# Row sums of relu(x): own semaphores, multi-row instructions and another split of memory in a kernel that streams 64 MB

## The chip, the cores and the metric

The kernel runs on one core of one Trainium2 chip. The metric is the device time of one execution in microseconds (us). A core has several engines with instruction queues of their own: ScalarE (ACT), VectorE (DVE), GpSimd (POOL), TensorE (PE, without work here) and SyncE (SP), which mostly issues DMAs. The transfers themselves are done by 16 DMA engines.

## The reference

```
x: float32 [32, 512, 1024]
relu_x = maximum(x, 0)
out    = sum(relu_x, axis=-1)      # float32 [32, 512]
```

There are 32 x 512 = 16384 rows of 1024 numbers, 4 KB each, 67.1 MB in all. Each row becomes one number: the sum of its positive parts.

## The kernel before

`trace_relu_sum` lays the rows over the 128 partitions so that partition p owns 128 rows that follow each other in memory (`xv`, `"(p m) d -> p (m d)"`). From one partition's data to the next one's it is 128 rows x 4 KB = 512 KB: the pitch. The rows of a partition are numbered m = 0 to 127.

They are loaded in pieces (`chunks`): seven blocks of 16 rows a partition (8.39 MB each), then a tail of 8, 4, 2 and 1 rows, and the last row (m = 127) in four column pieces of 244, 252, 260 and 268 numbers. All loads are issued by SP (line 95 for blocks and tail, line 121 for the pieces). The 16-row blocks and the 8-row tail share a pool of two buffers (tag `io`), so that a load waits until the block two before it has been worked off; the smaller ones have buffers of their own.

Each row is one instruction. Even rows go to ACT (`act_op`, line 71: Relu with an accumulated output), odd ones to DVE (`dve_op`, line 79: max with 0, then add, with an accumulated output). Both write one column of `res` (128 x 128). Each is followed by a short instruction that reads the accumulator. The four pieces of the last row are reduced by DVE; the first three sums are put behind the fourth piece's data, so that the fourth reduction gives the whole row.

The results leave in two stores: columns 0 to 125 from ACT's queue (line 103), and the last two columns from SP (line 128), at the end.

The tile framework places all semaphores and the closing: at the end (its instructions carry line 16) SP waits for the outstanding DMAs, and then all engines pass a barrier, GpSimd clears the semaphores, and all engines pass a second barrier. `issue_ahead_of_the_barrier` moves the first load on SP (`EARLY = 1`) in front of the barrier with which the program opens.

Of the kernel before, what the change touches and what calls it, by code (L numbers as in the profile page):

```python
# [1 line left out]

# [4 lines left out]

EARLY = 1  # L10


def kernel(tc: tile.TileContext, x: bass.AP, out: bass.AP):
    trace_relu_sum(tc, x, out)
    tc.close()
    tc.compile()  # L16
    issue_ahead_of_the_barrier(tc, EARLY)


def issue_ahead_of_the_barrier(tc: tile.TileContext, n_loads: int):  # L20


    SP = mybir.EngineType.SP
    blocks = tc.nc.main_func.blocks
    opening = blocks[0].instructions
    body = next(b for b in blocks if b.name == tc.start_bb_name).instructions
    loads = [i for i in body if i.engine == SP][:n_loads]
    for i in loads:
        assert isinstance(i, mybir.InstDMACopy)
        body.remove(i)  # L30
    at = next(
        n
        for n, i in enumerate(opening)
        if i.engine == SP and isinstance(i, mybir.InstDrain)
    )
    opening[at:at] = loads


@with_exitstack
def trace_relu_sum(  # L40
    ctx: ExitStack,
    tc: tile.TileContext,
    x: bass.AP,
    out: bass.AP,
):
    nc = tc.nc
    fp32 = mybir.dt.float32

    P = nc.NUM_PARTITIONS
    x_flat = x.flatten_outer_dims()  # L50
    N, D = x_flat.shape
    assert N % P == 0
    NT = N // P

    xv = x_flat.rearrange("(p m) d -> p (m d)", p=P)
    out2d = out.rearrange("b s -> (b s)").rearrange("(p m) -> p m", p=P)

    big = 16
    tail = [8, 4, 2, 1]
    pieces = [244, 252, 260, 268]  # L60
    assert sum(pieces) == D
    nbig, rem = divmod(NT - sum(tail) - 1, big)
    assert rem == 0
    chunks = [big] * nbig + tail

    io_pool = ctx.enter_context(tc.tile_pool(name="io", bufs=2))
    res_pool = ctx.enter_context(tc.tile_pool(name="res", bufs=1))
    res = res_pool.tile([P, NT], fp32)

    def act_op(in_ap, out_ap, m):  # L70
        nc.scalar.activation(  # L71
            out=out_ap,
            in_=in_ap,
            func=mybir.ActivationFunctionType.Relu,
            accum_out=res[:, m : m + 1],
        )

    def dve_op(in_ap, out_ap, accum_out):
        nc.vector.tensor_scalar(  # L79
            out=out_ap,  # L80
            in0=in_ap,
            scalar1=0.0,
            scalar2=None,
            op0=mybir.AluOpType.max,
            op1=mybir.AluOpType.add,
            accum_out=accum_out,
        )

    m0 = 0
    for j, cpd in enumerate(chunks):  # L90
        if cpd >= 8:
            xt = io_pool.tile([P, cpd, D], fp32, tag="io", name=f"xt{j}")
        else:
            xt = io_pool.tile([P, cpd, D], fp32, tag=f"t{cpd}", bufs=1, name=f"xt{j}")
        nc.sync.dma_start(  # L95
            out=xt,
            in_=xv[:, m0 * D : (m0 + cpd) * D].rearrange("p (c d) -> p c d", c=cpd),
        )
        for c in range(cpd):
            m = m0 + c  # L100
            if m == NT - 2:
                act_op(xt[:, c, :], xt[:, c, :], m)
                nc.scalar.dma_start(out=out2d[:, 0 : NT - 2], in_=res[:, 0 : NT - 2])
            elif (c % 2) == 0:
                act_op(xt[:, c, :], xt[:, c, :], m)
            else:
                dve_op(xt[:, c, :], xt[:, c, :], res[:, m : m + 1])
        m0 += cpd

    m_last = m0  # L110
    assert m_last == NT - 1
    base = m_last * D
    np_ = len(pieces)
    wlast = pieces[-1] + (np_ - 1)
    ptiles = []
    col = 0
    for i, w in enumerate(pieces):
        shape_w = w if i < np_ - 1 else wlast
        pt = io_pool.tile([P, shape_w], fp32, tag=f"p{i}", bufs=1, name=f"p{i}")
        ptiles.append(pt)  # L120
        nc.sync.dma_start(out=pt[:, 0:w], in_=xv[:, base + col : base + col + w])
        col += w
    last = ptiles[-1]
    for i in range(np_ - 1):
        dve_op(ptiles[i], ptiles[i], last[:, pieces[-1] + i : pieces[-1] + i + 1])
    dve_op(last, last, res[:, m_last : m_last + 1])

    nc.sync.dma_start(out=out2d[:, NT - 2 : NT], in_=res[:, NT - 2 : NT])


# [1 line left out]
_INS = ['x']  # L132
_OUTS = [((32, 512), 'float32')]


# [23 lines left out]
```

## Time and profile before

| | us |
|---|---|
| median of 8 runs | 163.48 (163.25 to 163.70) |
| the profiled execution's own time | 163.87 |
| its span, from the first to the last instruction | 162.1 |
| DVE busy | 74.2 |
| ACT busy | 69.0 |
| POOL busy | 0.2 |
| a row on DVE (128x1024) | 1.215 each |
| a row on ACT (128x1024) | 1.043 each |

The span is shorter than the time of the execution it comes from, since something lies around the first and last instruction (here 1.77 us). Shares on the page are of the span. "q1" is the DMA queue that SP issues to, "q10" that of ACT, and "q14" brings instructions. The profiled execution is one execution; the median is that of unprofiled ones.

When the blocks have arrived can be read from the starts of the first ACT instruction of each, which waits for the transfer. These are lines of the trace's timeline, ACT alone (start, length, instruction, and in brackets how long the engine had been idle and what ended it):

```
22.36 1.06 ACT L71 ACTIVATE xt<-xt 128x1024 f32<-128x1024 f32 x1 [20.29 <-DMA xt<-in_x_dram]
41.69 1.06 ACT L71 ACTIVATE xt<-xt 128x1024 f32<-128x1024 f32 x1 [10.91 <-DMA xt<-in_x_dram]
61.59 1.06 ACT L71 ACTIVATE xt<-xt 128x1024 f32<-128x1024 f32 x1 [11.48 <-DMA xt<-in_x_dram]
80.97 1.06 ACT L71 ACTIVATE xt<-xt 128x1024 f32<-128x1024 f32 x1 [10.95 <-DMA xt<-in_x_dram]
100.82 1.06 ACT L71 ACTIVATE xt<-xt 128x1024 f32<-128x1024 f32 x1 [11.43 <-DMA xt<-in_x_dram]
120.17 1.06 ACT L71 ACTIVATE xt<-xt 128x1024 f32<-128x1024 f32 x1 [10.93 <-DMA xt<-in_x_dram]
139.53 1.06 ACT L71 ACTIVATE xt<-xt 128x1024 f32<-128x1024 f32 x1 [10.93 <-DMA xt<-in_x_dram]
149.24 1.06 ACT L71 ACTIVATE xt<-xt 128x1024 f32<-128x1024 f32 x1 [1.29 <-DMA xt<-in_x_dram]
```

### The profile page before, as it was taken

Reading aid. Unit: us, or ns where it says so; the run is one execution under the profiler, and the core shown is the slowest. Engines: PE = TensorE matmul, PEld = TensorE weight load, DVE = VectorE, ACT = ScalarE, POOL = GpSimd, SP = SyncE. Lnnn points to the kernel's source line nnn. Section 1 sums busy time; section 2 is a strip of 40 time slices with the busy share of each in tenths; the row PEclk is TensorE's granted clock in tenths of the full one; section 3 lists DMA queues with packets and bytes.
Section 4 is the critical chain, followed back from the end, with each engine's and each line's share of the span. In section 5 each row is a group of like instructions: output and inputs, shape, how many; then the busy total and the mean of one; then the engine's idle time right before and its main releaser. Section 6 shows DMA issues by size and latency. Waiting matters only on the chain.

```text
span 162.1 us, 347 instructions
## 1 busy us (share of the span) xinstructions
DVE 74.2 (46%) x134; ACT 69.0 (43%) x129; POOL 0.2 (0%) x4
## 2 busy tenths in 40 slices
DVE  0000049700795007940099201991039900598983
ACT  3000049500793007920099001990039700596882
POOL 0000000000000000000000000000000000000000
DMA  7996997997997998998998999999999997998980
GB/s 259 518 485 291 518 501 307 485 501 307 485 518 291 485 469 372 453 469 372 453 487 374 437 469 404 421 469 421 404 485 404 404 501 332 421 453 384 416 334 22
DMA packets 2450, 67.19 MB, mean 415 GB/s; under 512 B 528, under 2 KB 1040, under 8 KB 1168
## 3 DMA queue, kind: packets, MB, share of 16 engines
q1 hardware_dynamic: 2304, 67.11, 96.7%
q10 hardware_dynamic: 144, 0.06, 0.1%
q14 instruction: 2, 0.02, 0.0%
HBM read 67.11 MB, written 0.07 MB: 414 GB/s over the span
## 4 chain that ended last, share of the span: by engine, by line
DMA 79%; DVE 18%; SPq 1%; issue 0%; DVEq 0%
DMA xt<-in_x_dram 62%; DVE xt L79 17%; DMA p<-in_x_dram 17%; SPq L95 1%; DVE p L79 1%; DVEq L79 0%; DVEq L16 0%
## 5 line engine op out<-in xcount | busy, mean ns | idle before, releaser
L79 DVE TENSOR_SCALAR_CACHE_REDUCE xt<-xt 128x1024 f32<-128x1024 f32 x63 | 72.6, 1215 | 85.1 <-DMA xt<-in_x_dram 84.8
L71 ACT ACTIVATE xt<-xt 128x1024 f32<-128x1024 f32 x64 | 66.7, 1043 | 89.6 <-DMA xt<-in_x_dram 89.6
L71 ACT ACTIVATION_READ_ACCUMULATOR xt<-xt 128x1 f32 x64 | 12.0, 187 | 0.0
L79 DVE DVE_READ_ACCUMULATOR xt<-xt 128x1 f32 x63 | 5.2, 83 | 0.0
L79 DVE TENSOR_SCALAR_CACHE_REDUCE p<-p 128x244 f32<-128x244 f32 (+3 forms) x4 | 1.6, 420 | 0.4 <-DMA p<-in_x_dram 0.4
L71 ACT ACT_TABLE_LOAD x1 | 1.3, 1283 | 0.8 <-PEq L143 0.8
L79 DVE DVE_READ_ACCUMULATOR p<-p 128x1 f32 x4 | 0.3, 82 | 0.0
L143 POOL MEMSET const-bfloat16-1.0<- 128x1 bf16 x1 | 0.1, 101 | 0.0
L143 POOL MEMSET const-uint8-127<- 128x1 uint8 x1 | 0.1, 101 | 0.0
L143 POOL MEMSET const-float32-0.0<- 128x1 f32 x1 | 0.1, 98 | 0.2 <-issue 0.2
L143 POOL MEMSET const-float32-1.0<- 128x1 f32 x1 | 0.1, 98 | 0.0
## 6 DMA issues: line engine op xcount, KB each, us to landing
xt<-in_x_dram SPq DMA_DIRECT2D x1, 4096.0 KB, 19.7
xt<-in_x_dram SPq DMA_DIRECT2D x1, 2048.0 KB, 24.2
xt<-in_x_dram SPq DMA_DIRECT2D x1, 1024.0 KB, 26.2
xt<-in_x_dram SPq DMA_DIRECT2D x1, 512.0 KB, 27.0
p<-in_x_dram SPq DMA_DIRECT2D x1, 134.0 KB, 10.0
p<-in_x_dram SPq DMA_DIRECT2D x1, 130.0 KB, 26.5
p<-in_x_dram SPq DMA_DIRECT2D x1, 126.0 KB, 26.7
p<-in_x_dram SPq DMA_DIRECT2D x1, 122.0 KB, 26.8
```

What stands on the lines that cost most here:

```text
L71: nc.scalar.activation(out=out_ap, in_=in_ap, func=mybir.ActivationFunctionType.Relu, accum_out=res[:, m : m + 1],)
L79: nc.vector.tensor_scalar(out=out_ap, in0=in_ap, scalar1=0.0, scalar2=None, op0=mybir.AluOpType.max, op1=mybir.AluOpType.add, accum_out=ac ...
L95: nc.sync.dma_start(out=xt, in_=xv[:, m0 * D : (m0 + cpd) * D].rearrange("p (c d) -> p c d", c=cpd),)
L143: nc = _bacc.Bacc("TRN2", target_bir_lowering=False, num_devices=1)
```

## The change

The computation stays the same; nearly the whole kernel is written anew.

- The framework's context is closed at once, and its body is filled with instructions that carry semaphores of the kernel's own: one for each of the 15 loads, one that ACT counts up, one that DVE counts up, and one for the stores.
- Memory is split in two. The first 2048 rows (8 MB) are the first block, in which a partition owns 16 rows (pitch 16 x 4 KB = 64 KB). The remaining 14336 rows are laid out with 112 rows a partition (pitch 448 KB). The loads keep their sizes: seven blocks of 16 rows, a tail of 8, 4, 2, 1, and four pieces.
- There are three buffers of 16 rows instead of two. The load of block j waits for DVE's count after block j-3; the tail's four loads share one buffer and only the first of them waits.
- Blocks 0 to 5 are worked off in multi-row instructions: ACT writes relu over n rows in place (`clamp`), then DVE sums these n rows with one `tensor_reduce` (`total`), which waits for ACT. The groups are 16, 16, 16, 8+8, 8+8, 6+5 rows. The other 5 rows of block 5 are single rows on ACT; block 6 is 8 single rows on ACT and 8 on DVE; the tail alternates as before.
- There are three stores, all on SP: the first block's 16 columns, then 110 columns, then the last two. The first two are issued after all loads in SP's program.
- At the end only GpSimd waits for the stores (semaphore at 48) and runs two of its closing instructions, among them the clear; the other closing instructions are dropped.

```diff
 def tile_relu_sum_kernel(tc: tile.TileContext, x: bass.AP, out: bass.AP):
-    trace_relu_sum(tc, x, out)
+    nc = tc.nc
+    sems = Semaphores(tc)
+
     tc.close()
     tc.compile()
+    nc.cur_bb = nc.bb_map[tc.start_bb_name]
+    body = nc.cur_bb.bb.instructions
+    ends = list(body)
+    body.clear()
+    n_stores = relu_sum(nc, sems, x, out)
+    body.extend(ends)
+
+    nc.cur_bb = nc.bb_map[tc.start_bb_name + "_end"]
+    body = nc.cur_bb.bb.instructions
+    clear = semaphore_clear(body)
+    body.clear()
+    nc.gpsimd.wait_ge(sems.stored, 16 * n_stores)
+    body.extend(clear)
     issue_ahead_of_the_barrier(tc, EARLY)
...
+TWO = [[16], [16], [16], [8, 8], [8, 8], [6, 5], []]
+ACT = [0, 0, 0, 0, 0, 5, 8]
+DVE = [0, 0, 0, 0, 0, 0, 8]
...
+    xf = x_flat[:N1].rearrange("(p m) d -> p m d", p=P)
+    xv = x_flat[N1:].rearrange("(p m) d -> p m d", p=P)
...
+    def store(m, n, act, dve):
+        nonlocal n_store
+        dst, src = sums(m, n)
+        nc.sync.wait_ge(sems.act, act)
+        nc.sync.dma_start(out=dst, in_=src).wait_op(sems.dve, dve, "sem-ge").then_inc(
+            sems.stored, 16
+        )
+        n_store += 1
+
+    def clamp(ap, loaded):
+        nonlocal n_act
+        i = nc.scalar.activation(out=ap, in_=ap, func=RELU)
+        if loaded is not None:
+            i.wait_op(loaded, 16, "sem-ge")
+        i.then_inc(sems.act, 1)
+        n_act += 1
+
+    def total(ap, m, n):
+        nonlocal n_dve
+        nc.vector.tensor_reduce(
+            out=res[:, m : m + n], in_=ap, axis=mybir.AxisListType.X, op=ADD
+        ).wait_op(sems.act, n_act, "sem-ge").then_inc(sems.dve, 1)
+        n_dve += 1
...
+    for j in range(NB):
+        buf = bufs[j % NBUF]
+        loaded = load(buf[:, :, :], rows(m, ROWS), j >= NBUF and freed[j - NBUF])
+        c = 0
+        act_waits = dve_waits = loaded
+        for n in TWO[j]:
+            clamp(buf[:, c : c + n, :], act_waits)
+            total(buf[:, c : c + n, :], m + c, n)
+            act_waits = None
+            c += n
+        for _ in range(ACT[j]):
+            act_row(buf[:, c, :], m + c, act_waits)
...
+        for _ in range(DVE[j]):
+            dve_row(buf[:, c, :], res[:, m + c : m + c + 1], dve_waits)
...
+        freed.append((n_act, n_dve))
...
+    store(0, ROWS, *freed[0])
+    store(ROWS, NT - ROWS - 2, n_act - 1, n_dve)
...
+    store(NT - 2, 2, n_act, n_dve)
+    return n_store
+
+
+def semaphore_clear(instructions):
+
+    pool = [i for i in instructions if i.engine == mybir.EngineType.Pool]
+    at = next(
+        n for n, i in enumerate(pool) if getattr(i, "is_reset_sema", False)
+    )
+    return pool[at : at + 2]
```

`act_row` and `dve_row` are the single-row instructions of before (`act_op`, `dve_op`), now with their own waits and counts.

## The prediction

> **What bounds the kernel now.** I read the page first (shares, queues, the chain that ended last), then the stream in stretches, then who waits for whom, then the end instruction by instruction.
>
> ```profile
> span 162.1 us, 347 instructions
> ...
> DVE 74.2 (46%) x134; ACT 69.0 (43%) x129; POOL 0.2 (0%) x4
> ...
> q1 hardware_dynamic: 2304, 67.11, 96.7%
> ...
> q14 instruction: 2, 0.02, 0.0%
> ...
> DMA 79%; DVE 18%; SPq 1%; issue 0%; DVEq 0%
> ```
>
> No compute engine is half busy; the queue of SyncE (q1) keeps the 16 DMA engines at 96.7% of the span. The 18% of VectorE in the chain is not compute time that bounds: those are the 16-row stretches after whose end a load is issued, and that load then only joins the end of a queue that is still full. The next view, busy time and traffic by stretch, shows it (columns: stretch, length, DVE busy, ACT busy, POOL busy, clock, DMA share, GB/s); the borders are the landings of blocks 0 to 3:
>
> ```profile
> 22.40:41.70 19.30, 9.17 (x17) 8.39 (x17) 0.00 (x0) 1.00 1.00 435
> 41.70:61.60 19.90, 9.19 (x16) 8.42 (x17) 0.00 (x0) 1.00 0.98 422
> 61.60:81.00 19.40, 9.20 (x16) 8.45 (x17) 0.00 (x0) 1.00 1.00 432
> ```
>
> A block of 8.39 MB takes 19.3 to 19.9 us and the engines are never out of work. The packet records of the same trace say why one block takes longer: a 64 KB packet takes 2.418 us nearly everywhere (27.1 GB/s an engine, 434 GB/s for 16), but about 50.5 us several engines lose some 0.4 to 0.5 us on one packet each, and the two 8 KB instruction fetches (q14 above) fall at 84.7 and 87.3 us, beside packets 0.28 and 0.54 us too long. The engine that lost at both 50.5 and 87.6 us is the last with the big blocks (138.94 us; the next is at 138.51), and the last load packet of all ends at 158.70.
>
> The end, from the timeline and from the instructions of line 16 (the closing of the tile context):
>
> ```profile
> 158.14 0.41 DVE L79 TENSOR_SCALAR_CACHE_REDUCE p<-p 128x244 f32<-128x244 f32 x1 [0.38 <-DMA p<-in_x_dram]
> ...
> 159.31 0.43 DVE L79 TENSOR_SCALAR_CACHE_REDUCE p<-p 128x271 f32<-128x271 f32 x1
> ...
> 159.81 0.35 SPq L128 DMA_DIRECT2D out_dram<-res  x1
> ```
>
> ```profile
> L16 SPq EVENT_SEMAPHORE  x7: 17/28/852, 160.2 to 162.0; - x7
> L16 POOLq EVENT_SEMAPHORE  x4: 17/17/17, 161.4 to 162.0; - x4
> L16 POOLq DRAIN  x3: 34/41/70, 0.7 to 161.8; - x3
> ...
> L16 POOLq EVENT_SEMAPHORE_RANGE_CLEAR  x1: 93/93/93, 161.7 to 161.7; - x1
> ```
>
> The reader is to see a string: last piece, four small reductions, store (issue 159.81, landing 1.4 us later, at 161.22), then 0.86 us to 162.08 in which SP, GpSimd and the others pass two rounds of drain and semaphores around one 93 ns clear.
>
> **What the Trainium skill says.** "DMA: Bandwidth & Descriptors", Where 436 GB/s comes from: 435.2 GB/s is the ceiling of the 16 ports. The trace agrees (435 in the first stretch): no layout can make the full stretches faster. The same page, Latency and other measured facts, has copies at a row pitch of 512 KiB a little below full rate (207 against 214 GB/s) and much below it only from 2 MiB up. This trace, with a pitch of 512 KB, runs at the ceiling, so that loss isn't here to be removed. "VectorE: DVE Perf Modes", The perf-mode tier table: `tensor_reduce` has only the 1x mode, so one element a cycle at 0.96 GHz. No reduce is in this trace; its tensor-scalar reductions agree with that rate (1024 / 0.96 = 1067 ns of the 1215). "ScalarE: Activation LUTs", What ACT_TABLE_LOAD costs, prices an ACTIVATE at 186 ns + 0.833 ns per element: 1039 ns for 1024, 1043 here.
>
> **The change, part by part.**
>
> *Loads.* Same bytes, same 15 loads, same 64, 32, 16, 8, 4 and 1 KB packets on the same queue, the first again ahead of the barrier. Before, SP's loads waited for VectorE and still came early:
>
> ```profile
> SPq L95 <- DVE xt L79: 126.4, 6, 30.5
> SPq L121 <- DMA xt<-in_x_dram: 16.3, 1, 16.3
> ```
>
> With three buffers and own semaphores these waits shrink or go; since the queue was never empty, worth 0. What replaces them: load j waits for the reduce of block j-3, and the tail's first load for that of block 4; behind a waiting load stand all later loads and the first store on SP. So the new compute order decides whether that stays harmless.
>
> *Compute.* A 16-row clamp on ACT: 0.19 + 16384 x 0.833 ns = 13.84 us; 8 rows 7.0, 6 rows 5.3, 5 rows 4.5. A 16-row reduce on DVE: 16384 / 0.96 = 17.07, plus the 0.15 fixed part of the 1215 ns row = 17.2 us; 8 rows 8.7, 6 rows 6.55, 5 rows 5.5. With today's landings (the first ACT starts: 22.36, 41.69, 61.59, 80.97, 100.82, 120.17, 139.53):
> block 0: ACT to 36.2, DVE to 53.5; block 1: 55.5, 72.8; block 2: 75.4, 92.7; from here DVE has no gap: block 3 to 110.1, block 4 to 127.4, block 5 (11 rows) to 139.5; ACT is done with block 5 at 135.1. Each reduce is a new wait of DVE for ACT; behind it in DVE's queue stands everything later, rows of block 6 and pieces included.
> Buffers come free at 53.5, 72.8, 92.7, 110.1 and 127.4, each 8 us or more ahead of the end of the last load already queued (61.6, 81.0, 100.8, 120.2, 139.5): loads stay hidden. Block 6 lands at 139.53 and finds DVE just free; its 8 DVE rows at 1.14 us (the spacing of rows at 149.28, 150.42, 151.56) end at 148.7, before the tail's landing at 149.24. DVE's gaps up to the first piece are then 0.59 + 0.2 + 0.2 + 0.38 = about 1.4 us. Cost: 0, with 1.4 us of cover. The unknown is the reduce: below, consecutive reduces may overlap their fixed parts (a gain in cover alone, never in time, as DMA bounds); above, every row beyond 1024 cycles costs 59 rows (blocks 2 to 5) times the excess, less 1.4 us. I take 0 excess; the upper end kept is 60 ns a row, 59 x 0.06 - 1.4 = +2.1 us.
>
> *Fewer instructions.* ACT falls from 64 row operations to 30 activations, DVE from 67 reductions to 28, so the fetches in mid-run should go: the last engine loses its 0.54, and the next one then sets the end (138.94 - 138.51): -0.4 us of the profiled execution. Bounds: 0 if other stray delays take their place, -1.0 if the 50.5 us loss goes as well (the latest engine would then end its big blocks at about 137.97).
>
> *Pitch.* 448 KB and 64 KB instead of 512 KB; at the port ceiling worth 0. The first packets alone took 2.9 to 3.5 us rather than 2.418; a contiguous first block could shorten or lengthen that: +-0.3, taken as 0.
>
> *Stores.* The big store moves from ACT to SP, in two. The first (rows 0 to 15) is issued behind the last piece at about 131 us, so in the rings it lies behind the loads; the second waits for the 4- and 2-row pieces' work, about 157.8, 0.35 us of SP; the third comes at 159.8, when SP is free again. ACT loses a 0.37 us issue that delayed its last row (158.27), which is off the path. 0.
>
> *End.* After the store's landing at 161.22 GpSimd passes its wait (17 ns plus a hand-over of some 50 ns, estimated from the spacing of those L16 rows), runs the 93 ns clear and one more short instruction (34 to 70 ns): done about 161.5 instead of 162.08, -0.6 us. Nothing is queued behind GpSimd. Bounds: -0.4 to -0.8, and 0 if what lies around the span (163.87 - 162.1 = 1.77 us) waits for something else.
>
> *Sum.* Profiled execution: 163.87 - 0.6 - 0.4 = 162.9. That execution lies 0.39 above the median of 163.48, probably by such stray delays, so part of the 0.4 is not in the median: I take 0.25 there. 163.48 - 0.6 - 0.25 = 162.6.
>
> **Rivals.** What can be told from no change here is about 0.2%, 0.33 us.
> - Forecast: port-bound as before, shorter end, one stray delay fewer: 162.6, range of its own 162.1 to 163.1. Chance 0.64.
> - The stream also loses the 50.5 us delay and starts quicker (contiguous first block): -0.6 - 0.6 - 0.3, 161.9. For it: the first wave's long packets; against: nothing ties either to the pitch. 0.14.
> - No change: the closing saved is waited for again outside the span, or a new stray delay eats it: 163.3. For it: 1.77 us outside that I can't read. 0.11.
> - Slower: the reduce. Place: DVE from 75 us on, no gap until block 6; price per row beyond 24 ns (1.4 us / 59) goes to the end one for one. At 60 ns: 163.48 + 2.1 - 0.6 = 165.0. For it: no reduce in the trace, cover of only 2% of a row; against: the 1x rate. 0.11.
>
> **Numbers.** Faster 0.78 (the first two), same 0.11, slower 0.11. The range goes from 161.6 (second case, with the -0.8 end) to 163.4 (all of the third).
>
> **What would show it.** After: ACT groups of about 13.8 us and DVE groups of about 17.2 us for 16 rows; block landings within 0.5 us of today's; the first piece's DVE operation still released by DMA; no q14 packets in mid-run; GpSimd's clear within 0.3 us of the last landing, as the last instruction. Wrong: DVE without a gap ahead of the pieces, a 16-row reduce above 17.6 us, SP loads landing late after a wait for DVE, or a span shorter by 0.6 with an unchanged time.

## The result, and the profile after

The changed kernel takes 162.32 us (median of 11 runs, 162.21 to 162.93), against 163.50 for the kernel before in the same comparison (30 runs, 163.25 to 163.87). The ratio is 0.9931, 95% interval 0.9922 to 0.9940. Its profiled execution took 162.24 us, with a span of 160.1.

The page of the changed kernel, the lines that answer to those shown of before:

```profile
span 160.1 us, 139 instructions
...
DVE 116.9 (73%) x47; ACT 102.8 (64%) x52; POOL 0.2 (0%) x4
...
q1 hardware_dynamic: 2592, 67.18, 97.9%
HBM read 67.11 MB, written 0.07 MB: 420 GB/s over the span
```

Both compute engines are far busier and there are fewer than half the instructions, but the kernel is still bound by the 16 DMA engines. The line of q14, the instruction fetches within the span, is gone. The stream by stretch, with the borders at the landings of blocks 0 to 4 (columns: stretch, length, DVE busy, ACT busy, POOL busy, clock, DMA share, GB/s):

```profile
21.90:41.25 19.35, 5.46 (x1) 13.86 (x2) 0.00 (x0) 1.00 1.00 434
41.25:60.60 19.35, 17.22 (x2) 13.86 (x1) 0.00 (x0) 1.00 1.00 434
60.60:79.95 19.35, 17.22 (x2) 13.86 (x1) 0.00 (x0) 1.00 1.00 434
79.95:99.30 19.35, 19.35 (x2) 13.95 (x3) 0.00 (x0) 1.00 1.00 434
```

Every one of these blocks takes 19.35 us; before, two took 19.90 and 19.85. Block 0 lands at 21.90 instead of 22.36. The two stretches and this first landing bring block 6 from 139.53 to 138.00, and the first piece's reduction from 158.14 to 156.79 us (-1.35). The end, from the timeline, from the instructions that carry line 105 (the three stores) with the issue and landing of the last store, and from those of line 29 (the closing):

```profile
156.79 0.41 DVE L137 TENSOR_SCALAR_CACHE_REDUCE piece<-piece 128x244 f32<-128x244 f32 x1 [0.45 <-DMA piece<-in_x_dram]
...
157.99 0.43 DVE L205 TENSOR_SCALAR_CACHE_REDUCE piece<-piece 128x271 f32<-128x271 f32 x1
```

```profile
L105 SPq DMA_DIRECT2D out_dram<-res x3: 332/344/5002, 129.9 to 158.5; - x3
...
out_dram<-res SPq DMA_DIRECT2D x1, 1.0 KB, 1.4
```

```profile
L29 POOLq DRAIN  x1: 88/88/88, 159.9 to 159.9; - x1
L29 POOLq EVENT_SEMAPHORE_RANGE_CLEAR  x1: 136/136/136, 160.0 to 160.0; - x1
```

The DMA still releases the first piece (0.45 us of idle DVE ahead of it). The last store is issued at 158.5 and lands 1.4 us later, as before; then a drain and the clear end the span at 160.12, about 0.3 us after the landing instead of 0.86. So the span of the profiled executions fell by 1.96 us, yet the time fell by 1.63 (163.87 to 162.24): what lies around the span rose from 1.79 to 2.12. Other runs agree: 1.74 to 1.84 in those of before, 2.07 to 2.16 in those of the changed kernel. The profiled execution of before is also the slowest of its 30 runs, so its trace shows more loss than the median contains.

### The profile page after: what moved, and what is told of

Same layout as the page of the kernel before. It is cut to its first block, busy times and chain, and to the rows that moved or that the text cites. A ratio compares the mean times of both kernels' runs of the same rounds, so it can differ in the third digit from the quotient of the medians.

```text
span 160.1 us, 139 instructions
## 1 busy us (share of the span) xinstructions
DVE 116.9 (73%) x47; ACT 102.8 (64%) x52; POOL 0.2 (0%) x4
## 4 chain that ended last, share of the span: by engine, by line
DMA 43%; DVE 33%; ACT 17%; another core or an unknown queue 3%; SPq 1%; issue 0%
DVE res L120 32%; DMA io<-in_x_dram 25%; DMA piece<-in_x_dram 18%; ACT io L112 17%; SPq L94 1%; DVE piece L137 1%; DVE piece L205 0%
## 5 line engine op out<-in xcount | busy, mean ns | idle before, releaser
L120 DVE TENSOR_REDUCE res<-io 128x8 f32<-128x8192 f32 (+3 forms) x9 | 97.9, 10930 | 40.1 <-ACT io L112 40.1
L112 ACT ACTIVATE io<-io 128x8192 f32<-128x8192 f32 (+3 forms) x9 | 79.1, 8825 | 47.1 <-DMA io<-in_x_dram 47.1
L127 ACT ACTIVATE io<-io 128x1024 f32<-128x1024 f32 x21 | 21.9, 1045 | 6.9 <-DMA io<-in_x_dram 6.7
L137 DVE TENSOR_SCALAR_CACHE_REDUCE io<-io 128x1024 f32<-128x1024 f32 x15 | 17.4, 1216 | 1.0 <-DMA io<-in_x_dram 0.8
L127 ACT ACTIVATION_READ_ACCUMULATOR io<-io 128x1 f32 x21 | 3.9, 187 | 0.0
L137 DVE TENSOR_SCALAR_CACHE_REDUCE piece<-piece 128x244 f32<-128x244 f32 (+2 forms) x3 | 1.1, 414 | 0.4 <-DMA piece<-in_x_dram 0.4
L137 DVE DVE_READ_ACCUMULATOR io<-io 128x1 f32 x15 | 1.2, 83 | 0.0
```

The lines of the kernel that those rows point to most:

```text
L112: i = nc.scalar.activation(out=ap, in_=ap, func=RELU)
L120: nc.vector.tensor_reduce(out=res[:, m : m + n], in_=ap, axis=mybir.AxisListType.X, op=ADD).wait_op(sems.act, n_act, "sem-ge").then_inc(se ...
L127: i = nc.scalar.activation(out=ap, in_=ap, func=RELU, accum_out=res[:, m : m + 1])
L137: i = nc.vector.tensor_scalar(out=ap, in0=ap, scalar1=0.0, scalar2=None, op0=MAX, op1=ADD, accum_out=accum_out,)
```

## The experiments

Three questions were open: what each part is worth, why the stream itself got faster when its loads had never been late, and why 0.33 us appeared outside the span. The first four kernels each undo one thing.

**One pitch of 512 KB again.**

```diff
-    xf = x_flat[:N1].rearrange("(p m) d -> p m d", p=P)
-    xv = x_flat[N1:].rearrange("(p m) d -> p m d", p=P)
+    xv = x_flat.rearrange("(p m) d -> p m d", p=P)
...
     def rows(m, n):
-        if m < ROWS:
-            return xf[:, m : m + n, :]
-        return xv[:, m - ROWS : m - ROWS + n, :]
+        return xv[:, m : m + n, :]
```

> The changed kernel with memory laid out as before, 128 rows a partition at a pitch of 512 KB for all blocks; all else stays. Theory of the prediction (pitch worth 0, the stream got faster because of fewer instructions or by chance): 162.3 us, block 0 landing at 21.9, every full stretch 19.35. Rival (the pitch is what made block 0 land 0.46 us earlier and took the 0.5 us off the stretches of 19.9): block 0 at 22.3 or later, one or two stretches of 19.9, 162.8 to 163.4 us.

Measured: 162.92 us (162.75 to 163.11), ratio to before 0.9970 (0.9958 to 0.9982). Block 0 lands at 22.65, 0.75 later than in the changed kernel; ACT's first lines in the timeline:

```profile
0.78 1.28 ACT L104 ACT_TABLE_LOAD   x1 [0.78 <-PEq L251]
22.65 13.86 ACT L104 ACTIVATE io<-io 128x16384 f32<-128x16384 f32 x1 [20.58 <-DMA io<-in_x_dram]
41.95 13.86 ACT L104 ACTIVATE io<-io 128x16384 f32<-128x16384 f32 x1 [5.44 <-DMA io<-in_x_dram]
```

In its packet records, eight 64 KB packets at 11.3 to 12.2 us took 2.67 to 2.93 us instead of 2.418, and the last packet of the first wave (the first packet of each of the 16 engines) ended at 5.06 us (changed kernel 4.62). Within an engine each packet begins where the one before it ended, so the packets of block 0 can be put together into 16 chains: the last chain ends at 22.28 us (changed kernel 21.52), and the last one without a long packet already at 21.97. So 0.45 of the 0.76 comes from the first wave and the rest from the group. After block 0 all stretches are 19.3 to 19.4. So the pitch costs 0.6 us in this kernel, and the theory that it is worth 0 falls. Of the rival only the place differs: the loss lies in block 0 rather than in a later stretch.

**The closing of before again.**

```diff
-    clear = semaphore_clear(body)
-    body.clear()
-    nc.gpsimd.wait_ge(sems.stored, 16 * n_stores)
-    body.extend(clear)
+    closing = list(body)
+    body.clear()
+    nc.sync.wait_ge(sems.stored, 16 * n_stores)
+    body.extend(closing)
```

> The changed kernel with the closing of before (SyncE waits for the stores, then barrier, clear, barrier). Theory of the prediction (the shorter closing is worth 0.6 us of the time): span 160.7, time 162.9. Rival (part of the saved closing is paid again outside the span, where 1.77 us became 2.14): span 160.7, time only 162.5, so a closing worth 0.2.

Measured: 163.02 us (162.87 to 163.28), ratio 0.9974 (0.9965 to 0.9984), span 160.75: +0.70 in time, +0.63 in the span. The time outside didn't fall back to 1.8 but rose to 2.16 to 2.39. So the short closing is worth its 0.6, and it is not what lengthened the time outside.

**One instruction a row.**

```diff
-TWO = [[16], [16], [16], [8, 8], [8, 8], [6, 5], []]
-ACT = [0, 0, 0, 0, 0, 5, 8]
-DVE = [0, 0, 0, 0, 0, 0, 8]
+TWO = [[], [], [], [], [], [], []]
+ACT = [8, 8, 8, 8, 8, 8, 8]
+DVE = [8, 8, 8, 8, 8, 8, 8]
...
     def load(dst, src, after=None):
...
+        if after:
+            nc.sync.wait_ge(sems.act, after[0])
```

In the multi-row form each reduce waits for ACT, so DVE's count covers ACT's work on the buffer. Here it doesn't, so a load waits for ACT's count too. The same wait is in the kernels with all three undone, with the new closing alone put back and with two buffers.

> The changed kernel with one instruction a row in blocks 0 to 5 too (8 rows on ACT, 8 on DVE, as in block 6); layout, buffers, stores and closing stay. Theory of the prediction (mid-run instruction fetches delayed the last DMA engine, 0.4 us): packets of q14 in mid-run again, one or two stretches of up to 19.9 us, 162.5 to 162.8. Rival (pitch or chance, fetches do nothing): 162.3, all full stretches 19.35.

Measured: 162.61 us (162.43 to 162.84), ratio 0.9952 (0.9939 to 0.9965). Two instruction packets are back (page), and one stretch is longer (stretches by landing):

```profile
q14 instruction: 2, 0.02, 0.0%
```

```profile
41.45:60.81 19.36, 9.20 (x16) 8.43 (x16) 0.00 (x0) 1.00 1.00 433
60.81:80.56 19.75, 9.21 (x17) 8.43 (x17) 0.00 (x0) 1.00 0.99 426
80.56:99.91 19.35, 9.21 (x17) 8.43 (x17) 0.00 (x0) 1.00 1.00 434
```

The reader is to see that the long stretch is the one with the fetches: they run at 67.05 and 67.09 us for 0.31 us each, and the load packets that start at 67.35 and 67.40 take 0.42 and 0.58 us more than 2.418. The load packets before them end where the fetches begin, so a fetch and the longer packet behind it hold up one DMA engine by 0.73 and 0.89 us. The block is complete only when its last engine is; it comes 0.40 us later, so the two engines had some slack. The span is 0.56 longer than the changed kernel's, but the time outside is 1.83 to 1.94 instead of 2.07 to 2.16, which leaves +0.29.

**DVE's cover taken away.**

```diff
-TWO = [[16], [16], [16], [8, 8], [8, 8], [6, 5], []]
-ACT = [0, 0, 0, 0, 0, 5, 8]
+TWO = [[16], [16], [16], [8, 8], [8, 8], [8, 8], []]
+ACT = [0, 0, 0, 0, 0, 0, 8]
```

> The changed kernel with all 16 rows of block 5 as two clamps and two reduces of 8 rows, so five more rows on DVE and five fewer on ACT. Theory of the prediction (DVE has no gap from block 3 on and about 1.3 us of cover up to the first piece; every us beyond goes to the end): 5 x 1.067 = 5.3 us more on DVE, less 1.3, so +4.0: 166.3 us, and no idle time of DVE ahead of the first piece. Rival (the cover is larger than the groups show, since DMA sets the end): under 163 us.

Measured: 165.46 us (165.26 to 165.83), ratio 1.0128 (1.0110 to 1.0145). From DVE's timeline, two lines of block 5's reduces and block 6's first row, and one from the first piece:

```profile
126.04 17.27 DVE L120 TENSOR_REDUCE res<-io 128x8 f32<-128x8192 f32 x2
143.23 1.22 DVE L137 TENSOR_SCALAR_CACHE_REDUCE io<-io 128x1024 f32<-128x1024 f32 x1
```

```profile
160.32 0.41 DVE L137 TENSOR_SCALAR_CACHE_REDUCE piece<-piece 128x244 f32<-128x244 f32 x1
```

The same place in the changed kernel:

```profile
74.49 63.44 DVE L120 TENSOR_REDUCE res<-io 128x16 f32<-128x16384 f32 x7 [2.13 <-ACT io L112]
138.00 1.22 DVE L137 TENSOR_SCALAR_CACHE_REDUCE io<-io 128x1024 f32<-128x1024 f32 x1
```

Without the cover, block 6 had landed at 138.05 and DVE reached it only at 143.23; the first piece's line has no idle time in brackets, so DVE bounds the end. DVE is 5.3 us later after block 5 (143.23 instead of 137.93, where the seven reduces above end) and the last reduction 3.5 us later (161.45 instead of 157.99): the cover was 1.8 us, not 1.3. The four idle stretches of DVE had been added up right (1.3 to 1.4 us). What was left out is that each of them also breaks the overlap of a row's end with the next row's start (1.22 us long, 1.14 apart, so 0.08 each), and that DVE waits 0.07 us ahead of block 6 and starts its second piece 0.06 us later than it does without cover (0.39 after the first instead of 0.33). Of the 3.5 us the time shows 3.1, since the time outside the span is shorter here (1.86 to 1.93 us).

The next four ask whether the three parts are the whole gain, which of the two pitches matters, and where the time outside comes from.

**All three undone together** (the three diffs above in one kernel; what is left are own semaphores, the third buffer and the stores on SyncE).

> The changed kernel with the pitch of 512 KB, the closing of before and one instruction a row, all three undone together; what is left of the change is its own semaphores, three buffers and the three stores on SyncE. Theory (these three undone parts make up the whole gain; own semaphores, third buffer and stores are worth 0): 163.4 to 163.6 us, several engines losing 0.3 to 0.5 us at one place in some block, mid-run instruction packets. Rival (the third buffer or the own semaphores carry a part): under 163.1.

Measured: 163.35 us (163.02 to 163.61, 21 runs), ratio 0.9994 (0.9986 to 1.0001): not to be told from the kernel before. Its packets show both losses, a group of long ones at 11.4 to 12.1 us and two long ones behind fetches at 64.9 and 67.3. Time outside: 1.74 to 1.83, as before. Own semaphores, the third buffer and the stores are worth nothing together; they were not taken apart.

**The contiguous block last, and every block contiguous.** In the first, `N1` is the first 112 rows of each partition and the last 16 lie at 64 KB; in the second all blocks do:

```diff
-    xf = x_flat[:N1].rearrange("(p m) d -> p m d", p=P)
-    xv = x_flat[N1:].rearrange("(p m) d -> p m d", p=P)
+    xb = x_flat.rearrange("(b p m) d -> b p m d", p=P, m=ROWS)
```

> The changed kernel with the contiguous 8 MB (64 KB pitch) as its last 16 rows instead of its first; blocks 0 to 6 have the pitch of 448 KB. If the 64 KB pitch makes the first block start quicker: block 0 lands at 22.3 to 22.6 instead of 21.90, 162.7 us. If the power-of-two pitch of 512 KB is what costs and any other pitch does: block 0 at 21.9 to 22.0, 162.3 us, no packets of 2.8 us.

> The changed kernel with every 16-row block contiguous (64 KB pitch throughout), and the first store over seven blocks. If only the first block's start matters: as the changed kernel, 162.3, block 0 at 21.9, stretches 19.35. If the 64 KB pitch is itself a cost in mid-stream: stretches above 19.5 and over 162.7. If 448 KB still costs something that 64 KB does not: under 162.1.

Measured: 162.26 us (162.10 to 162.40), ratio 0.9919 (0.9905 to 0.9933), block 0 at 22.04; and 162.26 us (162.25 to 162.79), ratio 0.9931 (0.9917 to 0.9945), block 0 at 21.73. No 64 KB packet behind the first wave takes over 2.55 us in either. So it is neither the contiguous start nor the 448 KB as such: any of these layouts does, and 512 KB doesn't. Neither is distinguishably better than the changed kernel.

**Padding: 90 more instructions on ACT and 91 on DVE**, in the 20 us in which both wait for block 0.

```diff
+    nc.vector.memset(scratch[:, 0:PAD], 0.0).then_inc(sems.pad, 1)
+    for i in range(PAD):
+        nc.vector.memset(scratch[:, 2 * PAD + i : 2 * PAD + i + 1], 0.0)
+    for i in range(PAD):
+        k = nc.scalar.activation(
+            out=scratch[:, PAD + i : PAD + i + 1], in_=scratch[:, i : i + 1], func=RELU
+        )
+        if i == 0:
+            k.wait_op(sems.pad, 1, "sem-ge")
```

> The changed kernel with 91 small fills of a scratch tile on DVE and 90 activations of one column on ACT in the first 20 us, while both wait for block 0; nothing else changes. Theory (the time outside the span rose from 1.78 to 2.11 us because the instructions that close the execution are fetched after the span, where the longer program of before had them fetched in mid-run): the time outside falls to 1.8 to 1.9, two q14 packets appear within the span, one or two engines lose 0.4 there, time 162.2 to 162.5. Rival (outside has to do with something else): outside stays at 2.1, and the time at 162.3.

Measured: 162.51 us (162.48 to 162.65), ratio 0.9942 (0.9929 to 0.9954). The two instruction packets are within the span again, at 6.7 and 9.1 us, with packets 0.53 and 0.24 too long behind them; block 0 lands at 22.54. The time outside fell from 2.11 to between 1.85 and 1.92. So in this pair of kernels, which differ in the padding alone, the fetches cost the stream, and without them the end takes longer, as the theory had it. The time outside is 1.74 to 1.94 us in all six kernels with fetches within the span and 2.06 to 2.39 in seven of the eight without. The trace of the kernel with the old closing recorded an 8 KB instruction packet at 162.89, 2.1 us after its span's end (the view of the DMA queues from 160 to 164 us):

```profile
q14 instruction: 1, 0.01, 0.6%
```

That this packet brings the instructions which close the execution fits, but isn't shown: the changed kernel's trace ends before such a packet, and the kernel without cover is an exception, with no fetch in its span and only 1.86 to 1.93 outside. How the closing is fetched stays open. Shown is that 181 more instructions lower the time outside by 0.2 us; that the program's length is all there is to it is not, since the kernel without cover has fewer instructions than the changed one.

**A pitch of 256 KB, and the new pitch alone in the kernel before.**

```diff
-    xf = x_flat[:N1].rearrange("(p m) d -> p m d", p=P)
-    xv = x_flat[N1:].rearrange("(p m) d -> p m d", p=P)
+    xh = x_flat.rearrange("(h p m) d -> h p m d", p=P, m=H)
```

> The changed kernel with memory in two halves of 64 rows a partition, pitch 256 KB for both; all else stays. If every large power of two as pitch brings the group of packets of 2.7 to 2.95 us that both kernels with 512 KB showed: such a group in some block and 162.7 to 163.0 us. If it takes 512 KB or more: no such group, first wave started by 1.9 us, 162.3.

> The kernel before with the new split of memory alone (first 8 MB at 64 KB, the rest at 448 KB; ACT's store becomes two). If the pitch is worth its 0.6 us by itself: 162.8. If it and the mid-run instruction fetches overlap, since only the latest DMA engine counts: 163.0 to 163.3, no group of long packets, but two long ones beside the fetches.

Measured: with 256 KB 162.34 us (162.18 to 163.06), ratio 0.9948 (0.9933 to 0.9963), block 0 at 21.90, no group of long packets: the trace shows nothing of what it shows at 512 KB. The ratio is less clear, since it lies between those of the changed kernel (0.9931) and of 512 KB (0.9970), and its interval meets both; a loss of a few tenths isn't excluded. The kernel before with the split alone: 163.14 us (162.92 to 163.58), ratio 0.9990 (0.9982 to 0.9998); block 0 at 21.86, no group, but fetches at 83.97 and 84.13 with packets 0.36 and 0.61 too long, and a stretch of 20.06. So the split by itself gives only about 0.2 us where the fetches are still there.

**Two buffers instead of three** (`NBUF = 2`).

> The changed kernel with two buffers of 16 rows instead of three; loads wait for ACT's count too. Worked out from the changed kernel's groups (clamp 13.86, reduce 17.22, a block 19.35 us on the queue): load 2 can only be issued at 53.0, lands at 73.8, load 4 at 125.7, load 6 at 170.9, and the end follows block 6 by 22.1: 195 us. If the third buffer isn't needed: 162.3.

Measured: 198.58 us. The queue runs dry, as two stretches show, from the landing of block 1 to that of block 2:

```profile
41.16:55.00 13.84, 11.78 (x1) 13.84 (x1) 0.00 (x0) 1.00 0.23 76
55.00:74.90 19.90, 17.22 (x1) 0.02 (x2) 0.00 (x0) 1.00 0.98 422
```

Load 2 comes at 52.9, when the reduce of block 0 ends, and lands at 74.90; blocks 4 and 6 land at 128.00 and 174.39, each a little later than worked out, since a load issued to an empty queue lands 22.0 us later (52.94 to 74.90), 2.6 more than a block behind another, where the expectation had taken 1.5. With multi-row instructions the third buffer is a condition; with row instructions (all three undone) it was worth nothing together with the own semaphores and the stores.

**The new closing alone, put back into the kernel with all three undone.**

> The kernel of e5 (own semaphores, three buffers, one instruction a row, 512 KB) with the new closing alone put back: GpSimd waits for the stores and clears. If the closing is worth its 0.6 us of span in a long program too: 0.6 below e5, 162.75 us, time outside the span 1.8 to 1.9. The kernel with one instruction a row and the new pitch (162.61) then lies 0.1 to 0.2 lower, the pitch's share beside the fetches. Rival (the barriers dropped are paid again outside the span): 163.3, outside 2.3.

Measured: 162.77 us (162.63 to 163.14), ratio 0.9950 (0.9932 to 0.9969), time outside 1.83 to 1.92. This closes a path from the kernel before to the changed one, one part a step. The kernels were measured in different comparisons, in which the median of the kernel before was 163.31 to 163.61; the column "difference" is to the median of the kernel before in the same comparison, and steps are read from it.

| kernel | median us | difference | ratio | span of the profiled execution | outside, its runs |
|---|---|---|---|---|---|
| before | 163.50 | 0 | 1 | 162.1 | 1.74 to 1.84 |
| own semaphores, three buffers, stores on SyncE | 163.35 | -0.09 | 0.9994 | 161.4 | 1.74 to 1.83 |
| + new closing | 162.77 | -0.84 | 0.9950 | 160.9 | 1.83 to 1.92 |
| + new pitch | 162.61 | -0.82 | 0.9952 | 160.7 | 1.83 to 1.94 |
| + multi-row instructions (the changed kernel) | 162.32 | -1.18 | 0.9931 | 160.1 | 2.07 to 2.16 |

The closing's step of -0.75 stands clear of the runs' spread (the intervals of its two ratios are apart). The pitch's step is nil, although undoing the pitch alone costs 0.67 by the same measure (-0.51 against -1.18, intervals apart). The kernel with one pitch is the missing corner of a square, all four with the new closing (difference, and interval of the ratio):

| | one instruction a row | multi-row instructions |
|---|---|---|
| pitch 512 KB | -0.84 (0.9932 to 0.9969) | -0.51 (0.9958 to 0.9982) |
| new split | -0.82 (0.9939 to 0.9965) | -1.18 (0.9922 to 0.9940) |

Neither the pitch nor the multi-row instructions gain anything alone that can be told; the last 0.35 us comes from both together. The interval with both stands apart from the one above it, but just touches the one beside it, so this rests on the four values together and on the spans. The spans of the four profiled executions say why: from 160.91 us the pitch alone leads to 160.68 and the multi-row instructions alone to 160.80, but both to 160.12. One delay is only seen when the other is gone, which fits that the last of the 16 engines counts. In the time, the multi-row instructions then give 0.2 to 0.3 back outside the span.

## Why the prediction was right, point by point

It forecast 162.6 us and a gain of 0.9; the gain was 1.18. What bounds the kernel, the cover and the closing were right in their mechanism. Two terms were not, a pitch worth 0 and a fixed time outside the span; they err in opposite directions, and that they cancel in part is luck.

- *Bound by the ports, stretches at the ceiling.* Right: 434 GB/s in the first four stretches after, 422 to 434 in the same stretches before, and DVE's 73% changes nothing.
- *Compute and cover.* A 16-row clamp was put at 13.84 us and took 13.86, a 16-row reduce at 17.2 and took 17.22, an 8-row one at 8.7 and took 8.67. The Trainium skill's rate for `tensor_reduce` in "VectorE: DVE Perf Modes", The perf-mode tier table (1x), holds: (17.22 - 8.67) / 8192 elements is 1.04 ns each, and no row costs extra, so the slower rival falls. That DVE's work beyond the cover goes to the end one for one was real, as the kernel without cover shows (5.3 us more work, 3.5 us in the span); only the cover was 1.8 instead of 1.4 us.
- *Loads with three buffers, own semaphores, stores: 0.* Right together (ratio 0.9994, interval including 1).
- *End: -0.6.* Right: -0.75 in the step on the path, 0.70 when undone alone.
- *Fewer instructions: -0.4 of the profiled execution, of which 0.25 in the median with the stray delays.* The step measured -0.36, close to the 0.25, but as the sum of two terms of which the prediction had one: about -0.56 in the span (no engine is held up by a fetch), and +0.2 to +0.3 outside, where the time had been taken as fixed at 1.77. And it measured this only with the new pitch in place. The argument, which held the pitch for worth nothing, should give the same saving at 512 KB; there the span of the profiled execution fell by 0.1 and the time not at all (the square above). So the number of this term came out by luck.
- *Pitch: 0.* This is the term that was mis-sized: 0.6 us once the fetches are gone. The argument was that the full stretches run at the ceiling, where no layout helps. That holds for the stretches, but not for the engine that is last. At 512 KB all four profiles (before, the single undoing, all three undone, the closing put back) have one group of 6 to 8 packets of 2.6 to 2.96 us, at 50, 11, 11 and 26 us, and a first wave that ends at 5.03 to 5.11 us. No other profile without a queue run dry has such a group, and their first waves end at 4.44 to 4.85. The group at 50.5 us that the prediction saw and called stray belonged to the layout. One packet of before of the same length, at 64.57 us, stands beside neither the group nor a fetch, so the two causes don't cover every delay. What the pitch is worth depends on what else delays the last engine: 0.6 us without fetches in the stream, 0.2 or nothing with them (0.17 in the kernel before with the split alone, nothing on the path). The second case of the prediction (the stream loses that delay too and starts quicker, 161.9) is what happened in the span: the big blocks end at 137.51 us instead of 138.94, earlier than the 137.97 that the prediction gave as the bound, because the first wave is earlier as well; its "nothing ties either to the pitch" fell, and the time outside took part of it back.

The Trainium skill's "DMA: Bandwidth & Descriptors", Latency and other measured facts, was cited for a pitch of 512 KiB being a little slow (207 against 214 GB/s, measured on copies between HBM tensors). In this stream it isn't a lower rate: a packet takes 2.418 us at 512, 448, 256 and 64 KB alike, and the loss is one group of packets and the first wave, 0.6 of 160 us. Why that group comes once, and in block 0, 1 or 2, stays open, as does why the first wave is later.

## What to carry to other kernels

When a stream runs at the ceiling, its end is set by the one DMA engine that was delayed most: look for single long packets and what stands beside them (instruction fetches, a group that comes with one layout), and expect such losses to overlap rather than add: here removing either of two delays alone gained nothing, so each was to be judged with the other one gone. A shorter program moves an instruction fetch out of the stream, but can lengthen what follows the span, so the time and the span must be read side by side. Dropped barriers at the end are worth what the trace shows behind the last landing, here 0.6 us.

## What the runs showed of the hardware that had not been expected

- An instruction fetch of 8 KB takes 0.31 us on one DMA engine, but the 64 KB load packet behind it takes 0.24 to 0.62 us longer than its 2.418, so the engine loses 0.55 to 0.93 us in all.
- The time outside the span isn't a constant of the core: 1.74 to 2.39 us by program here, steady to about 0.1 within all but one (the old closing with multi-row instructions).
- A row pitch of 512 KB costs this stream up to 0.6 us, in one profile 0.45 of 0.76 us in the first packets; at 64 KB no such loss was seen, and at 256 KB none in the trace, though its ratio leaves room for a few tenths.
